# Four gated FFNs on one core: the second pair of chunks of each done whole like the first, x's sums cut into pieces, norms and low parts queued ahead of a step's evacuation

## The chip, the cores and the metric

The program runs on one core of a Trainium2 chip. The metric is the device time of one execution in microseconds (us). The engines of the core are TensorE (PE, with its weight loads shown as PEld), VectorE (DVE), ScalarE (ACT), GpSimd (POOL) and SyncE (SP), which issues the loads of the weights. Each engine works through its own queue in the order in which the program wrote it.

## The reference, cut to what matters

Two blocks of two layers each are computed on 512 tokens of width 1024. The change touches only the four gated FFNs of the second block:

```python
def rmsnorm_2(x, g, eps=EPS):
    y = x * lax.rsqrt(jnp.mean(x * x, axis=-1, keepdims=True) + eps)
    return y * g

def swiglu(h, w_gate, w_up, w_down):           # h: 512 x 1024, w_gate, w_up: 1024 x 2816
    return (jax.nn.silu(h @ w_gate) * (h @ w_up)) @ w_down

for layer in range(2):
    ...                                        # shared keys and values before layer 1
    x = x + 0.5 * swiglu(rmsnorm_2(x, ffn1_norm[layer]), ...)
    ...                                        # a recurrent block, or differential attention
    x = x + 0.5 * swiglu(rmsnorm_2(x, ffn2_norm[layer]), ...)
```

## The kernel before

x is kept transposed, in eight tiles of 128 features by 512 tokens (xT). Every fp32 operand of a product is split into a high part and a low part, and a product is three matmuls: high weights by high x, high weights by low x, low weights by high x (`fm`, L317 to L321). The high part of a weight block (wh) is a copy on ACT (L132), the low part (wl) a subtraction on DVE (L135). An FFN has 22 chunks of 128 hidden features, taken as 11 pairs, in the groups `PAIRS` of two, two, two, two and three pairs. The four FFNs have the keys a, b, c and d; each is one call of `swiglu`.

A pair can be done in two ways. Done **whole** (`sw_first`, pair 0 alone), each of its two chunks takes two products of 24 matmuls with 512 columns, one for the gate and one for the up weights; DVE multiplies the two results by the tokens' norm rB (L515), ACT takes the silu, DVE multiplies (L517), and ACT and DVE make the high and the low part of the result z (L518, L519). Done **in seven steps** (`step`, all other pairs), the 1024 inputs and the 512 tokens are halved, and seven products of 24 matmuls with 256 columns replace the eight of a plain product by halves (Winograd's form). Steps 1, 2, 4 and 5 read sums and differences of parts of x instead of x. `x_sums` makes these in four calls, on DVE (L482, L483, L487 to L489, L491, L492) and ACT (L484 to L486, L490), and in the kernel before all four stand in `sw_first`. The weights of steps 1, 2, 4 and 6 are sums too: one DVE addition of 128x1024 each (L454), then the copy on ACT, then the low part on DVE.

What each step leaves in PSUM is taken out right after it: for steps 0, 1 and 2 an ACT copy (`keep`, L574), for steps 3, 4 and 5 DVE operations (L582, L586, L588), for step 6 an ACT copy (L590). Steps 0, 2, 4 and 6 add up in one PSUM bank, so step 2 can't start before the copy of step 0 is out. When the seven are done, three things finish the pair (`end`): `scaled` (two DVE multiplications by rB, L600, each followed by an ACT silu, L601), `both` (a DVE product, L604, and the ACT copy that makes z's high part, L606) and `low` (z's low part on DVE, L609). They wait in the list `todo`; each following step takes one off after its matmuls are written.

Between the steps of a group stand the eight **downs** of the group before (`sw_down`): 12 matmuls with 512 columns each, then a DVE operation that adds the result to xT (L534). `sw_items` says after which steps they stand. The last group's downs (18 matmuls each) stand behind the last pair.

The weights come through one stream (`Stream`): `get` for an item splits the item two places on into its parts, from raw blocks that SP has loaded. With `late=True` the low part is not written to DVE's queue at once but kept in a list, which `flush` empties; in the kernel before a step and a down call `flush` after their evacuation, at their very end:

```python
            product(r, w, x, k0, c, s in (0, 1, 3), s in (3, 5, 6))
            if todo:
                todo.pop(0)()
            ...                       # evacuation of the step
            else:
                nc.scalar.activation(zf[:, :, 0, hi], q, AF.Copy)
                todo.extend(end(p, zf))
                todo.pop(0)()
            self.ws.flush()
```

## Time and profile before

| | us |
|---|---|
| median of 3 runs | 3972.29 (3971.31 to 3974.96) |
| profiled execution | 3975.06 |
| its span, on the core | 3973.3 |
| PE busy in the span | 3694.2 (93%) |
| DVE, ACT, POOL busy | 2670.4 (67%), 1604.9 (40%), 720.0 (18%) |

The four FFNs lie at 1930.04 to 2321.34 us of the span (a), 2505.91 to 2888.89 (b), 2980.82 to 3365.44 (c) and 3579.11 to 3963.27 (d); each from the first matmul of its first whole product to the end of its last down. The span is the core's time from its first instruction to its last; what the profiled execution adds to it is 1.8 us.

How to read the views: PE's matmuls overlap, so a matmul's own duration is longer than the distance to the next one, and lengths are taken here from start to start. An entry in square brackets in the order of time is the time that the engine sat idle before the row, and what ended it. In a row of a window the number behind each engine is its busy time in the stretch and in brackets its instructions; PEclk is the granted share of TensorE's clock.

### The profile page before, as it was taken

How to read it: one execution, taken by the hardware profiler on the slowest of the kernel's cores; microseconds unless marked ns; L12 is line 12 of the kernel's file. 1: busy time of each engine (PE TensorE's matmuls, PEld its weight loads, DVE VectorE, ACT ScalarE, POOL GpSimd, SP SyncE). 2: the span in 40 equal slices, each digit the busy share in tenths (PEclk: the TensorE clock that was granted, in tenths of full speed). 3: DMA queues.
4: the chain of work that ended last, by engine and by line, in shares of the span. 5: the costliest groups of instructions: out<-in, count | busy, mean ns of one | idle time of the engine just before them, and what ended most of it. 6: DMA issues, size and time to landing. Idle time of an engine off the chain costs nothing.

```text
span 3973.3 us, 55166 instructions
## 1 busy us (share of the span) xinstructions
PE 3694.2 (93%) x21404; PEld 3198.1 (80%) x21404; DVE 2670.4 (67%) x4329; ACT 1604.9 (40%) x2642; POOL 720.0 (18%) x755
## 2 busy tenths in 40 slices
PE   7999989999999879999899988899998999998998
PEld 5887978888877778887688866788877888677887
DVE  7887787665554395444677767677756776766775
ACT  2454422222234484233344445444434444564443
POOL 5433230000021282000100034000030000550000
PEclk8999999999999999999899999999999999899999
DMA  5300043344413532333233323233353333213332
GB/s 180 95 1 22 14 130 116 111 127 121 120 50 105 156 110 78 94 89 92 66 103 95 93 67 90 75 96 96 96 152 88 96 98 99 75 48 88 96 96 77
DMA packets 586147, 367.72 MB, mean 93 GB/s; under 512 B 34487, under 2 KB 563373, under 8 KB 585885
## 3 DMA queue, kind: packets, MB, share of 16 engines
q1 hardware_dynamic: 564573, 348.31, 29.9%
q0 software_dynamic: 3520, 9.59, 0.8%
q10 hardware_dynamic: 17792, 6.29, 0.7%
q8 instruction: 169, 2.77, 0.3%
q14 instruction: 93, 0.76, 0.1%
HBM read 347.82 MB, written 16.30 MB: 92 GB/s over the span
## 4 chain that ended last, share of the span: by engine, by line
PE 64%; DVE 19%; ACT 7%; issue 6%; DMA 3%; POOL 1%; SPq 0%; DVEq 0%; ACTq 0%; POOLq 0%
PE D L1483 6%; PE D L317 5%; PE D L319 5%; PE D L321 5%; DVE wl L135 5%; PE D L551 3%; PE D L549 3%; PE D L550 3%; PE M L531 3%; PE M L532 3%; PE M L530 3%; PE V L1928 2%; DVE ws L454 2%; ACT wh L132 2%; PE E L549 2%
## 5 line engine op out<-in xcount | busy, mean ns | idle before, releaser
L135 DVE TENSOR_TENSOR wl<-ws,wh 128x1024 fp32r<-128x1024 f32 (+3 forms) x502 | 621.4, 1246 | 269.2 <-ACT wh L132 268.2
L132 ACT ACTIVATE wh<-ws 128x1024 fp32r<-128x1024 f32 (+3 forms) x502 | 486.7, 984 | 722.0 <-DVE ws L454 399.0
L551 PE MATMUL D<-ah,wl 128*128 128x256 f32 x1440 | 411.2, 286 | 48.9 <-DVE wl L135 48.0
L549 PE MATMUL D<-ah,wh 128*128 128x256 f32 x1440 | 407.3, 283 | 13.8 <-ACT t L574 13.8
L550 PE MATMUL D<-al,wh 128*128 128x256 f32 x1440 | 405.6, 282 | 0.0
L551 PEld LDWEIGHTS D<-ah,wl 128*128 128x128 f32 x1440 | 273.7, 190 | 58.8 <-DVE wl L135 58.8
L530 PE MATMUL M<-hz,wh 128*128 128x512 f32 x704 | 282.3, 401 | 8.6 <-ACT hz L606 8.6
L549 PEld LDWEIGHTS D<-ah,wh 128*128 128x128 f32 x1440 | 273.9, 190 | 20.2 <-ACT t L574 16.3
L531 PE MATMUL M<-hz,wh 128*128 128x512 f32 x704 | 282.5, 401 | 2.7 <-DVE hz L609 2.7
L532 PE MATMUL M<-hz,wl 128*128 128x512 f32 x704 | 281.8, 400 | 0.0
L550 PEld LDWEIGHTS D<-al,wh 128*128 128x128 f32 x1440 | 273.7, 190 | 4.1
L341 POOL TENSOR_TENSOR acc<-acc,t 128x512 f32<-128x512 f32 x36 | 46.9, 1302 | 1233.7 <-ACT t L340 1233.7
L549 PE MATMUL E<-ah,wh 128*128 128x256 f32 x800 | 227.2, 284 | 19.2 <-ACT t L574 9.7
L551 PE MATMUL E<-ah,wl 128*128 128x256 f32 x800 | 229.0, 286 | 14.1 <-DVE wl L135 13.5
L550 PE MATMUL E<-al,wh 128*128 128x256 f32 x800 | 225.9, 282 | 0.0
L303 POOL TENSOR_TENSOR hl<-t,hh 128x768 fp32r<-128x768 f32 (+1 forms) x44 | 69.2, 1573 | 811.0 <-ACT hh L302 770.1
L317 PE MATMUL D<-ah,wh 128*128 128x512 f32 (+1 forms) x512 | 205.8, 402 | 6.4 <-DVE G L797 4.2
L321 PE MATMUL D<-ah,wl 128*128 128x512 f32 (+1 forms) x512 | 203.9, 398 | 2.5 <-DVE wl L135 2.5
L319 PE MATMUL D<-al,wh 128*128 128x512 f32 (+1 forms) x512 | 203.7, 398 | 0.3 <-POOL al L2625 0.2
L1300 DVE SCALAR_TENSOR_TENSOR as<-ws,S,as 128x256 f32<-128x256 f32 x448 | 198.5, 493 | 4.9 <-DMA ws<-in_ada_w_dram 1.4
L317 PE MATMUL D<-x7h,wh 128*128 128x512 f32 (+1 forms) x464 | 183.5, 398 | 3.0 <-ACT x7h L2620 1.6
L319 PE MATMUL D<-x7l,wh 128*128 128x512 f32 (+1 forms) x464 | 181.9, 395 | 1.0 <-POOL x7l L2625 0.5
(707 smaller groups left out, 9767.5 us busy)
## 6 DMA issues: line engine op xcount, KB each, us to landing
ws<-in_ffn_w_up_dram SPq DMA_DIRECT2D x96, 512.0 KB
ws<-in_ada_w_dram SPq DMA_DIRECT2D x88, 512.0 KB
t<-in_ffn_w_down_dram SPq DMA_DIRECT2D x128, 256.0 KB
ws<-in_ffn_w_gate_dram SPq DMA_DIRECT2D x80, 256.0 KB
ws<-in_ffn_w_up_dram SPq DMA_DIRECT2D x80, 256.0 KB
wz<-in_ffn_w_gate_dram SPq DMA_DIRECT2D x80, 256.0 KB
wz<-in_ffn_w_up_dram SPq DMA_DIRECT2D x80, 256.0 KB
ws<-in_ffn_w_down_dram SPq DMA_DIRECT2D x32, 384.0 KB
```

The source lines that it names most:

```text
L132: self.nc.scalar.activation(h[:, :n], t[:, :n], AF.Copy)
L135: self.nc.vector.tensor_tensor(l[:, :n], t[:, :n], h[:, :n], ALU.subtract)
L317: nc.tensor.matmul(o, wh[:, kw + k], xh[:, k0 + k, s], start=a, stop=False)
L319: nc.tensor.matmul(o, wh[:, kw + k], xl[:, k0 + k, s], start=False, stop=False)
L321: nc.tensor.matmul(o, wl[:, kw + k], xh[:, k0 + k, s], start=False, stop=z)
L530: nc.tensor.matmul(q, wh[:, k], z[:, 0, i], start=k == 0, stop=False)
L531: nc.tensor.matmul(q, wh[:, k], z[:, 1, i], start=False, stop=False)
L532: nc.tensor.matmul(q, wl[:, k], z[:, 0, i], start=False, stop=k == 2 * np_ - 1)
L549: nc.tensor.matmul(o, wh[:, u, k], xh(k0 + k, s), start=start and k == 0, stop=False, skip_group_check=True)
L550: nc.tensor.matmul(o, wh[:, u, k], xl(k0 + k, s), start=False, stop=False, skip_group_check=True)
L551: nc.tensor.matmul(o, wl[:, u, k], xh(k0 + k, s), start=False, stop=stop and k == 3, skip_group_check=True)
L1483: nc.tensor.matmul(o, w[u][:, k], hs[m0 + k][h][:, s], start=k == 0 and i == 0, stop=k == nm - 1 and i == 2)
```

## The change

Pairs 0 and 1, the whole first group, are done by `sw_first`; `sw_first` takes the pair as an argument. One call of `x_sums` belongs to each chunk of the two pairs. It is a generator now, and its three pieces are written at three places of the chunk: the first behind the gate product, the second behind the silu, the third behind the ACT copy of z's high part. Its scratch tile moves from a ring that the downs' weights use to the tile of the norm's diagonal. `flush` moves ahead of the evacuation, in the step and in the down. `scaled` is no longer taken off `todo` at the end of step 6, so that `scaled`, `both` and `low` come one step later each, in steps 0, 1 and 2 of the next pair; the buffer gu is asked for at step 3. In a group's second pair the first down stands behind step 0 and no longer behind step 1.

```diff
-                if p0 + q == 0:
+                if not gi:
                     for m in range(2):
-                        yield "g", 0, m
-                        yield "u", 0, m
+                        yield "g", q, 2 * q + m
+                        yield "u", q, 2 * q + m
                     continue
                 for s in range(7):
                     yield "s", p0 + q, s
-                    if down and s in ((2, 3, 5, 6), (1, 2, 4, 6))[q]:
+                    if down and s in ((2, 3, 5, 6), (0, 2, 4, 6), ())[q]:
                         yield down.pop(0)
...
     def x_sums(self, d, n):
-        t = self.tmp(TT, tag="ca", bufs=3)
+        t = self.tmp(TT, tag="diag", bufs=1)
         nc.vector.tensor_scalar(ng, gb, -1.0, None, ALU.mult)
         nc.vector.tensor_tensor(f, a0, a1, ALU.subtract)
         nc.scalar.activation(e, a1, AF.Copy, scale=g)
         nc.scalar.activation(f, f, AF.Copy, scale=g)
         nc.scalar.activation(th[:, 0:TC], f, AF.Copy)
+        yield
         nc.vector.scalar_tensor_tensor(t[:, TC:2 * TC], b1, gb, e, ALU.mult, ALU.subtract)
         nc.vector.scalar_tensor_tensor(t[:, 0:TC], b1, ng, f, ALU.mult, ALU.subtract)
         nc.vector.scalar_tensor_tensor(t[:, 2 * TC:], b0, ng, t[:, 0:TC], ALU.mult, ALU.subtract)
+        nc.vector.tensor_tensor(tl[:, 0:TC], f, th[:, 0:TC], ALU.subtract)
         nc.scalar.activation(th[:, TC:], t, AF.Copy)
-        nc.vector.tensor_tensor(tl[:, 0:TC], f, th[:, 0:TC], ALU.subtract)
+        yield
         nc.vector.tensor_tensor(tl[:, TC:], t, th[:, TC:], ALU.subtract)
...
-    def sw_first(self, key, d):
+    def sw_first(self, key, d, p):
...
-                self.fm([(q[:, i], slice(0, T))], self.ws.get((key, kind, 0, m)), d.x)
+                self.fm([(q[:, i], slice(0, T))], self.ws.get((key, kind, p, 2 * p + m)), d.x)
...
-                if m == 0 and i == 0:
-                    d.t = self.acts512()
-                else:
-                    self.x_sums(d, 2 * m + i - 1)
+                if not i:
+                    if not p and not m:
+                        d.t = self.acts512()
+                    x = self.x_sums(d, 2 * p + m)
+                    next(x)
             nc.vector.tensor_tensor(zf[:, :, m], q, d.rB.unsqueeze(1).to_broadcast([P, 2, T]), ALU.mult)
             nc.scalar.activation(zf[:, 0, m], zf[:, 0, m], AF.Silu)
+            next(x)
             nc.vector.tensor_tensor(zf[:, 1, m], zf[:, 0, m], zf[:, 1, m], ALU.mult)
             nc.scalar.activation(z[:, 0, m], zf[:, 1, m], AF.Copy)
+            next(x, None)
             nc.vector.tensor_tensor(z[:, 1, m], zf[:, 1, m], z[:, 0, m], ALU.subtract)
-        self.x_sums(d, 3)
         return z
...
     def sw_down(self, key, gi, n, hs, scale):
+        self.ws.flush()
         x = self.xT[:, n]
         nc.vector.scalar_tensor_tensor(x, q, scale, x, ALU.mult, ALU.add)
...
         def step(p, s, banks):
             if s == 0:
-                un[p] = dict(z=self.gu())
+                un[p] = {}
...
             if todo:
                 todo.pop(0)()
-            zf, q = d_["z"], r[:, :, lo]
+            self.ws.flush()
+            if s == 3:
+                d_["z"] = self.gu()
+            zf, q = d_.get("z"), r[:, :, lo]
...
                 todo.extend(end(p, zf))
-                todo.pop(0)()
-            self.ws.flush()
```

The order of the built programs shows what this moves. DVE, FFN a, from the last whole chunk's multiplication by rB (L515 before, L519 after) to the first seven-step pair. wl is a low part, L454 a weight sum, al a low part of x's sums, hz a low part of z. Before:

```order
L515 TENSOR_TENSOR gu_16686<-D_16789,rB_16765 128x2x512
L517 TENSOR_TENSOR gu_16686<-gu_16686 128x512
L519 TENSOR_TENSOR hz_16685<-gu_16686,hz_16685 128x512
L482 TENSOR_SCALAR t_16881<-VC 128x1
L483 TENSOR_TENSOR t_16882<-xT 128x256
L487 SCALAR_TENSOR_TENSOR t_16884<-xT,VC,t_16883 128x256
L488 SCALAR_TENSOR_TENSOR t_16884<-xT,t_16881,t_16882 128x256
L489 SCALAR_TENSOR_TENSOR t_16884<-xT,t_16881,t_16884 128x256
L491 TENSOR_TENSOR al_16734<-t_16882,ah_16733 128x256
L492 TENSOR_TENSOR al_16734<-t_16884,ah_16733 128x768
L135 TENSOR_TENSOR wl_16835<-ws_73,wh_16834 128x1024
L454 TENSOR_TENSOR ws_73<-ws_73,wz_16684 128x1024
```

After, behind the last chunk of pair 1:

```order
L519 TENSOR_TENSOR gu_16869<-E_16953,rB_16767 128x2x512
L489 SCALAR_TENSOR_TENSOR t_16984<-xT,VC,t_16983 128x256
L490 SCALAR_TENSOR_TENSOR t_16984<-xT,t_16981,t_16982 128x256
L491 SCALAR_TENSOR_TENSOR t_16984<-xT,t_16981,t_16984 128x256
L492 TENSOR_TENSOR al_16728<-t_16982,ah_16727 128x256
L522 TENSOR_TENSOR gu_16869<-gu_16869 128x512
L495 TENSOR_TENSOR al_16728<-t_16984,ah_16727 128x768
L525 TENSOR_TENSOR hz_16868<-gu_16869,hz_16868 128x512
L135 TENSOR_TENSOR wl_16993<-wz_16682,wh_16992 128x1024
L454 TENSOR_TENSOR wz_16682<-wz_16682,ws_74 128x1024
```

Behind the last L515 of before stood one whole call of `x_sums` after z's low part, and ahead of it in the same queue another; behind the last L519 of after stand two pieces of one call, among z's own operations. The low part L135 is that of step 1 of the first seven-step pair in both.

DVE, from the last evacuation of one seven-step pair (L588 before, L597 after) into the next pair, which is the first of its group (pair 3 into pair 4, FFN a). Before:

```order
L588 SCALAR_TENSOR_TENSOR gu_17444<-D_16897,t_17551 128x2x256
L600 TENSOR_TENSOR gu_17444<-gu_17444,rB_16765 128x2x512 x2
L135 TENSOR_TENSOR wl_17693<-ws_73,wh_17692 128x1024
L454 TENSOR_TENSOR ws_73<-ws_73,wz_16683 128x1024
L534 SCALAR_TENSOR_TENSOR xT<-M_17729,xT 128x512
L135 TENSOR_TENSOR wl_17727<-ws_73,wh_17726 128x1024
L454 TENSOR_TENSOR ws_73<-ws_73,wz_16684 128x1024
L604 TENSOR_TENSOR gu_17444<-gu_17444 128x1024
L135 TENSOR_TENSOR wl_17746<-ws_73,wh_17745 128x1024
```

After:

```order
L597 SCALAR_TENSOR_TENSOR gu_17504<-E_17032,t_17453 128x2x256
L135 TENSOR_TENSOR wl_17595<-wz_16682,wh_17594 128x1024
L454 TENSOR_TENSOR wz_16682<-wz_16682,wz_16683 128x1024
L135 TENSOR_TENSOR wl_17625<-wz_16682,wh_17624 128x1024
L540 SCALAR_TENSOR_TENSOR xT<-M_17627,xT 128x512
L454 TENSOR_TENSOR wz_16682<-wz_16682,ws_74 128x1024
L607 TENSOR_TENSOR gu_17504<-gu_17504,rB_16767 128x2x512 x2
L135 TENSOR_TENSOR wl_17644<-wz_16682,wh_17643 128x1024
L135 TENSOR_TENSOR wl_17678<-t_17538,wh_17677 128x512
L611 TENSOR_TENSOR gu_17504<-gu_17504 128x1024
```

The low parts of the next pair's steps 0 and 1 now stand ahead of the norms (L600 before, L607 after) and of the down's addition to xT (L534, now L540); the norms stand behind the weight sum of step 2.

ACT at the same place, from the copy of step 6 (L590, now L599) to the copy of step 0 (L574, now L583). Before:

```order
L590 ACTIVATE gu_17444<-D_16896 128x2x256
L601 ACTIVATE gu_17444<-gu_17444 128x512 x2
L132 ACTIVATE wh_17726<-ws_73 128x1024
L132 ACTIVATE wh_17745<-ws_73 128x1024
L606 ACTIVATE hz_17774<-gu_17444 128x1024
L574 ACTIVATE t_17776<-E_16898 128x512
```

After:

```order
L599 ACTIVATE gu_17504<-D_17031 128x2x256
L132 ACTIVATE wh_17624<-wz_16682 128x1024
L132 ACTIVATE wh_17643<-wz_16682 128x1024
L608 ACTIVATE gu_17504<-gu_17504 128x512 x2
L583 ACTIVATE t_17675<-D_17030 128x512
L132 ACTIVATE wh_17677<-t_17538 128x512
L613 ACTIVATE hz_17710<-gu_17504 128x1024
```

The copy of step 0 no longer stands behind the copy of z's high part (L606, now L613); the two silus stand ahead of it instead.

## Rows read from the trace of the kernel before

**Rows 1.** The page: PE's busy time, and its costliest group that waits.

```profile
PE 3694.2 (93%) x21404; PEld 3198.1 (80%) x21404; DVE 2670.4 (67%) x4329; ACT 1604.9 (40%) x2642; POOL 720.0 (18%) x755
L551 PE MATMUL D<-ah,wl 128*128 128x256 f32 x1440 | 411.2, 286 | 48.9 <-DVE wl L135 48.0
```

**Rows 2.** Windows, from:to and length: FFN a, one step, one whole product.

```profile
1930.04:2321.34 391.30, 360.41 (x2315) 323.01 (x2314) 289.59 (x355) 164.02 (x224) 14.64 (x14) 0.97 0.32 90
2077.50:2080.32 2.82, 2.82 (x25) 2.81 (x24) 1.82 (x2) 0.71 (x1) 0.00 (x0) 1.00 0.00 1
2980.82:2986.43 5.61, 5.61 (x26) 4.52 (x24) 1.21 (x2) 3.99 (x5) 0.00 (x0) 1.00 0.50 187
```

**Rows 3.** Windows: last whole product and pair 1's steps 0 to 2, FFNs a to d.

```profile
1958.55:1986.41 27.86, 15.99 (x98) 14.48 (x96) 20.70 (x32) 13.49 (x22) 0.00 (x0) 0.82 0.00 1
2524.53:2553.74 29.21, 17.71 (x97) 15.58 (x96) 21.40 (x34) 13.93 (x23) 0.00 (x0) 0.82 0.00 1
2998.53:3029.48 30.95, 18.68 (x97) 17.17 (x96) 22.12 (x35) 14.97 (x23) 0.00 (x0) 0.72 0.00 0
3597.74:3627.85 30.11, 16.39 (x97) 14.88 (x96) 21.40 (x34) 14.95 (x23) 0.00 (x0) 0.77 0.00 1
```

**Rows 4.** Windows: pair 2's steps 1, 2; pair 4's steps 0 to 2; pair 5's 0, 1.

```profile
2000.49:2009.17 8.68, 6.24 (x51) 5.83 (x49) 7.74 (x8) 5.19 (x7) 0.00 (x0) 1.00 0.05 15
2063.70:2074.70 11.00, 9.30 (x74) 8.67 (x72) 9.44 (x10) 5.61 (x7) 0.00 (x0) 1.00 0.06 17
2097.19:2103.93 6.74, 6.20 (x50) 5.79 (x49) 6.18 (x7) 2.56 (x4) 0.00 (x0) 1.00 0.11 34
```

**Rows 5.** In order of time, PE, FFN a: matmuls that waited (start, length).

```profile
1979.53 0.58 PE L551 MATMUL D<-ah,wl 128*128 128x256 f32 x1 [11.87 <-DVE wl L135]
...
2071.78 0.39 PE L549 MATMUL E<-ah,wh 128*128 128x256 f32 x1 [1.18 <-ACT t L574]
```

**Rows 6.** Groups by line, DVE, 1950 to 1979.5 us: x's sums.

```profile
L492 DVE TENSOR_TENSOR al<-t,ah 128x768 fp32r<-128x768 f32 x4 | 3.8, 958 | 2.3 <-ACT ah L490 2.3
...
L487 DVE SCALAR_TENSOR_TENSOR t<-xT,VC,t 128x256 f32<-128x256 f32 x4 | 1.9, 483 | 3.1 <-ACT t L484 3.1
...
L491 DVE TENSOR_TENSOR al<-t,ah 128x256 fp32r<-128x256 f32 x4 | 1.7, 418 | 0.0
```

**Rows 7.** In order of time, DVE, where pair 3 ends and pair 4 begins.

```profile
2061.73 1.23 DVE L600 TENSOR_TENSOR gu<-gu,rB 128x1024 f32<-128x1024 f32 x1 [1.15 <-ACT gu L590]
2062.87 1.22 DVE L135 TENSOR_TENSOR wl<-ws,wh 128x1024 fp32r<-128x1024 f32 x1
2064.12 1.22 DVE L454 TENSOR_TENSOR ws<-ws,wz 128x1024 f32<-128x1024 f32 x1
2065.26 0.68 DVE L534 SCALAR_TENSOR_TENSOR xT<-M,xT 128x512 f32<-128x512 f32 x1
2066.47 1.22 DVE L135 TENSOR_TENSOR wl<-ws,wh 128x1024 fp32r<-128x1024 f32 x1 [0.53 <-ACT wh L132]
2067.73 1.23 DVE L454 TENSOR_TENSOR ws<-ws,wz 128x1024 f32<-128x1024 f32 x1
2068.87 1.22 DVE L604 TENSOR_TENSOR gu<-gu 128x1024 f32<-128x1024 f32 x1
```

**Rows 8.** The same place, ACT.

```profile
2061.10 0.60 ACT L590 ACTIVATE gu<-D 128x512 f32<-128x512 f32 x1 [2.77 <-PE D L551]
2061.59 0.63 ACT L601 ACTIVATE gu<-gu 128x512 f32<-128x512 f32 x1
...
2068.99 1.06 ACT L132 ACTIVATE wh<-ws 128x1024 fp32r<-128x1024 f32 x1 [2.55 <-DVE ws L454]
2070.18 1.06 ACT L606 ACTIVATE hz<-gu 128x1024 fp32r<-128x1024 f32 x1
2071.15 0.58 ACT L574 ACTIVATE t<-E 128x512 f32<-128x512 f32 x1
```

**Rows 9.** Window around the end of FFN a's last pair.

```profile
2280.00:2295.00 15.00, 12.09 (x56) 9.67 (x56) 10.17 (x11) 5.52 (x8) 0.00 (x0) 0.89 0.28 80
```

More of the change, by code (lines that the diff above doesn't have):

```diff
@@ L615, in swiglu @@
         for kind, a, b in items:
-            if kind == "g" and b == 0:
-                hs[0] = self.sw_first(key, d)
-                three = [self.bank("D"), self.bank("D"), self.bank("E")]
+            if kind == "g" and b % 2 == 0:
+                hs[a] = self.sw_first(key, d, a)
+                if a == 1:
+                    three = [self.bank("D"), self.bank("D"), self.bank("E")]
             elif kind == "s":
@@ L630, in swiglu @@
                 self.sw_down(key, a, b, hs, 0.5)
-                self.ws.flush()
                 if a == last and on_x:
```

## The prediction

> **What bounds the kernel now.** I read the page first: PE is busy 93% of the span, and the costliest group of its matmuls that waits, waits for low parts of weights from DVE [rows 1]. So a change pays only where it shortens PE's own work or a wait of PE. Then I cut PE's order of time at the starts of the FFNs' products and took the windows. One step of 24 matmuls with 256 columns takes 2.82 us, one whole product of 24 with 512 columns 5.61 [rows 2]; a down of 12 with 512 columns is half of that, 2.81. Nearly everything in an FFN runs at these rates with nothing lost. What is lost lies at a few places, and I count it as window less its products at full rate:
>
> - Pair 0 into pair 1: each window holds one whole product and three steps, 5.61 + 3 x 2.82 = 14.06 us. They took 27.86, 29.21, 30.95 and 30.11 [rows 3]: lost 13.8, 15.15, 16.9 and 16.05, together 61.9. In FFN a 11.87 of it is one wait, for a low part [rows 5]. DVE is busy 20.70 of the 27.86 us and stood in a queue with two calls of x's sums. The rest, 13.8 - 11.9 = 1.9, comes after the wait: the granted clock of these windows is 0.72 to 0.82 of the full 2.4 GHz, so part of each ran at 1.2.
> - Pair 1 into pair 2: 8.68 for two steps [rows 4], lost 3.05.
> - Into the first pair of a group (pairs 4, 6, 8, and 10 likewise): 11.00 for three steps [rows 4], lost 2.55.
> - Into the second pair of a group (pairs 3, 5, 7, 9): 6.74 for two steps [rows 4], lost 1.11.
> - Behind the last pair PE waits for z: of 15 us it is busy 12.09, at 0.89 of the clock [rows 9].
>
> In the four FFNs that is 61.9 + 12.2 + 40.8 + 17.8 = 132.7 us, without starts and ends, which the change leaves alone.
>
> **Pair 1 whole.** Seven steps become four products: 4 x 5.61 - 7 x 2.82 = +2.7 us of PE per FFN, on the path, +10.8 in all. The bytes loaded are the same. Per column the two kinds of matmul cost the same here: a whole product has twice the columns of a step and takes 1.99 times as long [rows 2].
>
> The Trainium skill ("Perfetto Trace Analysis", Optimizing Tensor Performance) holds larger matmuls to be more efficient than smaller ones, and the Trainium skill ("TensorE: Matmul & The Clock Gate", Back-to-back issue gap) gives each a fixed cost of some 2.5 ns beside its columns; by these the charge would be some 2.4 us an FFN (an estimate: 96 x 215.8 - 168 x 109.2 ns), and the sum 1 us lower. The rows show 2.7, and decide.
>
> **x's sums in pieces.** A call has DVE operations of 0.96, 3 x 0.48 and 2 x 0.42 us [rows 6], near 3.3 with the small one, plus waits for ACT (2.3 and 3.1 in four calls). Before, four stood around two chunks; now one stands in each of four, 11.2 us of PE apiece. A chunk's DVE work is two low parts and the multiplication by rB at 1.22, two half ones at 0.69 and the 3.3: 8.4 of 11.2. So DVE keeps up and the loss of pair 0 into pair 1 goes: **-61.9**.
>
> What is late next is the end of pair 1. The low part for step 1 of pair 2 stands behind the last chunk's tail. DVE begins some 0.2 after PE goes on (a matmul lasts 286 ns [rows 1], the next starts 117 after it [rows 2]); multiplication by rB 1.13 (starts follow 1.13 to 1.14 apart [rows 7]), three sums and a low part 1.7 (3 x 0.48 + 0.42, overlapping a little), a product 0.6, then x's low part, which waits for an ACT copy of 768 columns (between 0.6 and 1.06 [rows 8]) and starts near 4.0 and z's low part at 4.9; the weight's low part runs 5.5 to 6.7. Step 1 wants it at 2.82 + 0.23 = 3.05: 3.6 lost. Then weight sum, copy and low part of step 2 (1.23 + 1.06 + 1.22 with 0.04 between) against another 3.05: 0.6 more. I take 4.3. In a and d step 0 needs the same bank as the last chunk and takes 1.5 of the same wait. After waits like these PE ran slower for a while (1.9 above, 0.89 in [rows 9]): 0 to 2, I take 1.4. So 5.7 in place of 3.05: **+10.5**. Bounds: 3 (what pair 2 loses now [rows 4]) and 7.1 (one more wait for ACT of [rows 6], 0.8, in the tail, and 2 for the clock).
>
> **Norms and low parts ahead.** Count from the start of step 0 of the next pair; durations from [rows 7, 8].
>
> *First pair of a group* (steps 0, 1, 2, then a down). The low parts of steps 0 and 1 are now done before step 0 begins. DVE: addition to xT at 0.2, weight sum of step 2 at 0.8, norms at 1.94 and 3.07, low part of step 2 from 4.2 to 5.4, wanted at 5.87. ACT: weight copy 2.06 to 3.12, silus to 3.83 and 4.96, copy of step 0 4.9 to 5.5; step 2 starts at 5.63 and needs it. Before, that copy stood behind z's high part (L606) and ended at 2071.73 [rows 8], and PE waited 1.18 for it [rows 5]. So nothing is lost here; z's low part (L604, copy, L609 behind that) comes at 15.9 and the down, which starts at 14.1, wants it with its eighth matmul at 15.7: 0.2 to 0.3 lost. 0.3 for 2.55, three times per FFN: **-27**. In the last pair, with no downs between its steps, step 6 wants the bank of step 4 2.8 us after step 4, and step 4's evacuation (2 x 0.42 on DVE) now stands behind step 6's weight sum, copy and low part; by the same count it comes 0.6 late. 0.7 for 2.55, four times: **-7.4**.
>
> *Second pair of a group* (0, down, 1, 2, down, 3, 4). The chain is the same to 5.4, but then come: weight sum of step 2 at 5.46, copy 6.72, low part 7.82 to 9.04, wanted at 8.67 (0.43 late). DVE: addition at 8.95, a down's low part, L604 10.15 to 11.37. ACT: z's high part to 12.47, copy of step 1 to 12.98, and only then the weight copy of step 3, to 13.95; its low part ends at 15.2, wanted at 14.8 (0.45). Sum, copy and low part of step 4 end at 18.7, wanted at 18.2 (0.57). With some 0.1 for starting again each time: 1.75 lost for 1.11, sixteen times: **+10**. The third down, moved behind step 0, is what covers step 1 here.
>
> The loads: raw blocks are given back at a flush, so no later than before; SP's queue gets nothing new, and the ring of the downs' weights loses x's sums as a user. I cost that at nothing; the DMA share over FFN a is 0.32 at 90 GB/s [rows 2]. The evacuations on DVE now stand behind a low part; elsewhere than in the last pair the bank of step 4 is wanted again 5.6 us on. Nothing too.
>
> **The sum.** -61.9 + 10.8 + 10.5 - 27 - 7.4 + 10 = -65 us. Against the profiled execution's 3975.06 (span 3973.3 and 1.8 around it) that gives 3910; this execution is 2.8 above the median of the runs, so the median should be 3972.3 - 65 = **3907**. The unknowns: the end of pair 1, 3 to 7.1 where I took 5.7 (-11 to +6); second pairs, 1.1 to 2.3 (-10 to +9); first pairs, 0 to 1.1 (-4 to +10). Not all fall on one side: 3892 to 3923 for this case.
>
> **The rivals.**
>
> - *The boundaries lose nothing.* ACT and DVE have slack over a pair (DVE is busy 289.59 of 391.30 us [rows 2]), and if the copies and low parts catch up the second pairs lose 0: 3907 - 28 - 4 - 3 = 3872. Against it: sum, copy and low part stand in series, 3.6 us, and a step has 2.82.
> - *The boundaries stay as they are.* The wait moves from one link to the next, first pairs lose 2.55 as now: 3907 + 27 + 7 - 10 = 3931. For it: the second pairs, where I find just that.
> - *The backlog moves to the end of pair 1.* If DVE can't keep up with x's pieces, pair 1 into pair 2 loses what pair 0 into 1 did, 15.5 for my 5.7: 3907 + 39 = 3946. Against it: 8.4 of 11.2.
> - *The blocks come late (slower).* The weight sums of steps 1 and 2 now stand ahead of the norms in DVE's queue. If a raw block is not in when its sum's turn comes, the norms, the silus and the copy of step 0 all stand behind it. The price is a block's load: 512 KB at the 187 GB/s of a busy stretch [rows 2] is some 2.8 us, an estimate, at 32 boundaries: 3907 + 90 = 3997. It decides when the block lands later than 0.8 us into step 0. No wait of that kind is in [rows 7]. The rows show DVE working in the written order, so nothing could pass the stalled sum.
> - *The change does nothing*, its order being undone when it is built: the order shows that it isn't. 3972.
>
> **How the numbers follow.** Forecast 0.72, boundaries free 0.08, boundaries as they are 0.08, backlog moved 0.07, late blocks 0.03, nothing 0.02. The range takes in the forecast's own and reaches to 3932, so that the boundaries as they are lie in it, and to 3889: some 0.2 is left out. A difference under 0.2% (8 us) can't be told from none here. Faster 0.95 (the first four), same 0.02, slower 0.03.
>
> **What the profile after would show.** Each FFN 14 to 19 us shorter, a near 377 for 391.3; no wait of 9 to 12 us of PE behind pair 0; a wait of 3 to 4 us, or of 1.5 and 2, at steps 0 and 1 of pair 2, with a lower clock behind it; no wait for the copy of step 0 (1.18 before) in pairs 4, 6 and 8; three waits of 0.4 to 0.6 for low parts at steps 2, 3 and 4 of pairs 3, 5, 7, 9. A wait over 5 us at pair 2 would make the pieces of x's sums wrong, DVE waiting for loads the last assumption, and waits of 2 us in pairs 4, 6, 8 the chain of norms.

## The result, and the profile after

The changed kernel took 3907.5 us (median of 4 runs, 3902.80 to 3910.74), the kernel before, on the same chip, 3971.8 (3969.15 to 3974.96): a ratio of 0.9837, 95% interval 0.982 to 0.9854. The forecast was 3907. The profiled execution has a span of 3904.1 us where before it was 3973.3: 69.2 less. The four FFNs, from the first matmul to the end of the last down, took 374.09, 367.93, 366.61 and 366.69 where they had taken 391.30, 382.98, 384.62 and 384.16: 67.7 of the 69.2 lie in them. One execution of e6_norms_only, at a granted clock of 0.75 where its others had 0.98, took 6378 us and is left out of its median below.

First the page of the kernel after, the lines that answer to [rows 1]:

```profile
PE 3693.3 (95%) x21116; PEld 3180.9 (81%) x21116; DVE 2622.7 (67%) x4293; ACT 1587.0 (41%) x2618; POOL 720.3 (18%) x755
L557 PE MATMUL D<-ah,wl 128*128 128x256 f32 x1344 | 382.6, 285 | 20.2 <-DVE wl L135 20.2
```

The same group of matmuls waits for the same low parts, 20.2 us in place of 48.0. PE's busy time is nearly the same: pair 1 whole adds work, and less time goes into slow running and into starting again behind waits, which count as busy ([rows 4] has 9.30 us busy for 8.45 of work).

Then windows of the kernel after (from:to, length, busy time of PE, PEld, DVE, ACT, POOL with their instructions, PEclk, DMA share, GB/s): FFN a; its last five whole products; then the last whole chunk's end to the end of step 2 of pair 2 in FFNs a, b, c and d.

```profile
1927.96:2302.05 374.09, 359.46 (x2243) 318.33 (x2242) 277.69 (x346) 159.27 (x218) 14.64 (x14) 0.99 0.33 94
1954.74:1982.83 28.09, 28.09 (x121) 22.41 (x119) 18.88 (x29) 13.58 (x21) 0.00 (x0) 1.00 0.46 122
...
1982.83:1995.67 12.84, 9.61 (x74) 8.83 (x74) 10.39 (x13) 5.62 (x8) 0.00 (x0) 1.00 0.08 24
...
2533.22:2546.66 13.44, 10.29 (x73) 10.08 (x72) 10.20 (x13) 5.71 (x8) 0.00 (x0) 0.87 0.12 36
2992.20:3006.70 14.50, 11.35 (x73) 11.14 (x72) 10.38 (x13) 5.71 (x8) 0.00 (x0) 0.76 0.18 54
3572.38:3585.14 12.76, 9.56 (x73) 8.80 (x73) 10.39 (x13) 5.61 (x8) 0.00 (x0) 1.00 0.07 21
```

The five products take 28.09 us, and five at the full rate are 5 x 5.61 = 28.05: nothing is lost where [rows 3] lost 13.8 to 16.9. DVE is busy 18.88 of the 28.09 and keeps up. Pair 2's steps 0 to 2 are 8.45 us at the full rate, so the boundary behind pair 1 loses 4.4, 5.0, 6.0 and 4.3. In a and d the granted clock is 1.00 and nearly all of it is waiting; in b and c it is 0.87 and 0.76, and 1.5 and 2.6 us of the loss are matmuls that ran at the lower level behind the wait.

Now a window of the second pair of a group (pair 3's steps 0 to 4 with the two downs between them), then two of the first pair of the next group (steps 0 to 2, and the down behind them), and one of the whole last pair (seven steps), all in FFN a:

```profile
2018.19:2039.66 21.47, 20.52 (x145) 18.81 (x144) 17.60 (x18) 9.91 (x13) 0.00 (x0) 1.00 0.20 58
...
2050.91:2059.42 8.51, 8.51 (x73) 8.51 (x72) 7.25 (x8) 3.93 (x6) 0.00 (x0) 1.00 0.06 17
2059.42:2062.46 3.04, 3.04 (x14) 2.18 (x13) 2.34 (x2) 2.90 (x5) 0.00 (x0) 1.00 0.73 212
...
2242.84:2263.35 20.51, 20.01 (x170) 19.84 (x168) 19.11 (x21) 10.34 (x13) 0.00 (x0) 1.00 0.05 16
```

The first pair loses 8.51 - 8.45 and 3.04 - 2.81, together 0.29, where [rows 4] had 2.55. The second pair loses 21.47 - (5 x 2.82 + 2 x 2.81) = 1.75, where it had 1.11. The last pair loses 20.51 - 7 x 2.815 = 0.8, where it had 2.55. The next rows show, in the order of time, PE's three waits in the second pair, DVE's chain there, and one piece of ACT's queue:

```profile
2027.28 0.38 PE L557 MATMUL D<-ah,wl 128*128 128x256 f32 x1 [0.26 <-DVE wl L135]
2033.40 0.39 PE L557 MATMUL D<-ah,wl 128*128 128x256 f32 x1 [0.24 <-DVE wl L135]
2036.94 0.39 PE L557 MATMUL D<-ah,wl 128*128 128x256 f32 x1 [0.46 <-DVE wl L135]
```

```profile
2019.00 1.22 DVE L454 TENSOR_TENSOR ws<-ws,wz 128x1024 f32<-128x1024 f32 x1
...
2022.40 1.22 DVE L135 TENSOR_TENSOR wl<-ws,wh 128x1024 fp32r<-128x1024 f32 x1
2023.65 1.23 DVE L454 TENSOR_TENSOR ws<-ws,ws 128x1024 f32<-128x1024 f32 x1
2026.00 1.23 DVE L135 TENSOR_TENSOR wl<-ws,wh 128x1024 fp32r<-128x1024 f32 x1 [1.12 <-ACT wh L132]
...
2032.12 1.23 DVE L135 TENSOR_TENSOR wl<-ws,wh 128x1024 fp32r<-128x1024 f32 x1 [0.21 <-ACT wh L132]
...
2035.66 1.23 DVE L135 TENSOR_TENSOR wl<-wz,wh 128x1024 fp32r<-128x1024 f32 x1 [1.18 <-ACT wh L132]
```

```profile
2029.60 1.06 ACT L613 ACTIVATE hz<-gu 128x1024 fp32r<-128x1024 f32 x1 [3.10 <-DVE gu L611]
2030.57 0.58 ACT L583 ACTIVATE t<-E 128x512 f32<-128x512 f32 x1
2031.04 1.05 ACT L132 ACTIVATE wh<-ws 128x1024 fp32r<-128x1024 f32 x1
```

Step 0 began at 2018.19. From there step 1's weight sum runs at 0.81 and its low part at 4.2, the weight sum of step 2 at 5.46, its low part at 7.81 and ends at 9.04: the prediction's count to within a hundredth. ACT makes z's high part before the weight copy of step 3, which is the second wait. Each low part ends a few hundredths before the matmul that wanted it.

### The profile page after: what moved, and what is told of

Same layout as the page of the kernel before. It is cut to its first block, busy times and chain, and to the rows that moved or that the text cites. A ratio compares the mean times of both kernels' runs of the same rounds, so it can differ in the third digit from the quotient of the medians.

```text
span 3904.1 us, 54600 instructions
## 1 busy us (share of the span) xinstructions
PE 3693.3 (95%) x21116; PEld 3180.9 (81%) x21116; DVE 2622.7 (67%) x4293; ACT 1587.0 (41%) x2618; POOL 720.3 (18%) x755
## 5 line engine op out<-in xcount | busy, mean ns | idle before, releaser
L135 DVE TENSOR_TENSOR wl<-ws,wh 128x1024 fp32r<-128x1024 f32 (+3 forms) x474 | 586.7, 1246 | 324.4 <-ACT wh L132 322.4
L132 ACT ACTIVATE wh<-ws 128x1024 fp32r<-128x1024 f32 (+3 forms) x474 | 457.3, 978 | 571.4 <-DVE ws L454 256.8
L557 PE MATMUL D<-ah,wl 128*128 128x256 f32 x1344 | 382.6, 285 | 20.2 <-DVE wl L135 20.2
L317 PE MATMUL D<-ah,wh 128*128 128x512 f32 (+1 forms) x616 | 246.0, 399 | 3.1 <-ACT wh L132 2.8
L321 PE MATMUL D<-ah,wl 128*128 128x512 f32 (+1 forms) x616 | 243.1, 395 | 2.8 <-DVE wl L135 2.8
L319 PE MATMUL D<-al,wh 128*128 128x512 f32 (+1 forms) x616 | 243.2, 395 | 0.3 <-POOL al L2632 0.2
L303 POOL TENSOR_TENSOR hl<-t,hh 128x768 fp32r<-128x768 f32 (+1 forms) x44 | 69.2, 1573 | 808.4 <-ACT hh L302 767.5
L557 PE MATMUL E<-ah,wl 128*128 128x256 f32 x672 | 189.9, 283 | 4.1 <-DVE wl L135 4.1
L555 PE MATMUL E<-ah,wh 128*128 128x256 f32 x672 | 188.9, 281 | 2.9 <-DVE gu L519 2.8
L556 PE MATMUL E<-al,wh 128*128 128x256 f32 x672 | 188.3, 280 | 0.0
L321 PE MATMUL D<-x7h,wl 128*128 128x512 f32 (+1 forms) x464 | 181.4, 394 | 1.1 <-DVE wl L135 1.1
```

The lines of the kernel that those rows point to most:

```text
L132: self.nc.scalar.activation(h[:, :n], t[:, :n], AF.Copy)
L135: self.nc.vector.tensor_tensor(l[:, :n], t[:, :n], h[:, :n], ALU.subtract)
L317: nc.tensor.matmul(o, wh[:, kw + k], xh[:, k0 + k, s], start=a, stop=False)
L319: nc.tensor.matmul(o, wh[:, kw + k], xl[:, k0 + k, s], start=False, stop=False)
L321: nc.tensor.matmul(o, wl[:, kw + k], xh[:, k0 + k, s], start=False, stop=z)
L555: nc.tensor.matmul(o, wh[:, u, k], xh(k0 + k, s), start=start and k == 0, stop=False, skip_group_check=True)
```

## The experiments

Each kernel ran with the kernel before on the same chip; ratios are to that.

| kernel | what it is | median us | ratio, 95% interval |
|---|---|---|---|
| after | the change | 3907.5 | 0.9837 (0.982 to 0.9854) |
| e1_whole | only pair 1 whole and x's pieces | 3929.6 | 0.9887 (0.9874 to 0.9901) |
| e2_order | only the reordering | 3946.7 | 0.9929 (0.9917 to 0.9942) |
| e3_old_places | after, the downs where they were | 3874.5 | 0.9751 (0.9738 to 0.9765) |
| e4_uncut | after, x's sums not cut | 3914.8 | 0.9848 (0.9835 to 0.9862) |
| e5_low_parts_only | e3, norms where they were | 3910.1 | 0.9837 (0.9824 to 0.985) |
| e6_norms_only | e3, low parts where they were | 3894.1 | 0.9799 (0.9785 to 0.9812) |
| e7_x_early | e3, x's sums ahead of the last tail | 3869.6 | 0.9745 (0.9732 to 0.9758) |
| e8_tail_later | e7, the last tail put off | 3858.6 | 0.9711 (0.9698 to 0.9724) |
| e9_down_moved_alone | before, the one down moved | 3961.2 | 0.9968 (0.9956 to 0.9979) |
| e10_last_pair | e8, the last pair by halves | 3861.0 | 0.9718 (0.9705 to 0.9731) |
| e11_last_pair_woven | e10, halves woven | 3841.9 | 0.9671 (0.9658 to 0.9685) |

**The two halves of the change.** My theory was the prediction's own: the gain is the sum of separate boundaries. The first experiment takes the reordering out:

```diff
-                    if down and s in ((2, 3, 5, 6), (0, 2, 4, 6), ())[q]:
+                    if down and s in ((2, 3, 5, 6), (1, 2, 4, 6), ())[q]:
...
             product(r, w, x, k0, c, s in (0, 1, 3), s in (3, 5, 6))
             if todo:
                 todo.pop(0)()
-            self.ws.flush()
...
                 todo.extend(end(p, zf))
+                todo.pop(0)()
+            self.ws.flush()
```

> Only the first half of the change: pair 1 whole and x's sums in pieces; norms, low parts and the third down stand where the kernel before has them. My theory counts the two halves apart: this one keeps -61.9 + 10.8 + 10.5 and gives back 27 + 7.4 - 10 = 24.4 against the changed kernel (3907.5): 3932. Its trace: no loss between pairs 0 and 1, first pairs of a group again 2.5 over their products, second pairs 1.1. Rival A, the reordering of norms and low parts does nothing: 3907. Rival B, the two halves need each other (without the early low parts the pieces of x's sums pile up at the end of pair 1): over 3950.

It took 3929.6. Windows of its pair 3 (steps 0, 1) and pair 4 (steps 0 to 2):

```profile
2021.35:2028.10 6.75, 6.17 (x50) 5.76 (x49) 6.19 (x7) 2.55 (x4) 0.00 (x0) 1.00 0.14 41
2053.40:2064.41 11.01, 9.25 (x74) 8.64 (x73) 9.44 (x10) 5.62 (x7) 0.00 (x0) 1.00 0.04 13
```

6.75 and 11.01 stand where [rows 4] has 6.74 and 11.00: these boundaries are untouched, and pair 0 into pair 1 loses nothing. The second one keeps the reordering and does pair 0 alone whole, with x's sums as before:

```diff
-                if not gi:
+                if p0 + q == 0:
...
-                    x = self.x_sums(d, 2 * p + m)
-                    next(x)
+                else:
+                    self.x_sums(d, 2 * m + i - 1)
```

> Only the second half: norms and low parts ahead of a step's evacuation and the third down of a second pair behind step 0; pair 0 alone is whole and x's sums are called as before. Theory: 3972 - 24 to 28 (the boundary of pairs 1 and 2 is now a first pair of its kind and gains 1 to 1.5 us in each FFN as well) = 3944 to 3948, with 13 to 17 us still lost between pairs 0 and 1. Rival A (the reordering does nothing): 3972. Rival B (the early low part of step 1 also breaks the wait between pairs 0 and 1): 3925 or less.

It took 3946.7, as expected. The gains alone, 1.13% and 0.71%, add to 1.84%, the change has 1.63%. At the boundary of pairs 1 and 2 the reordering gains some 1.5 us an FFN in e2, where pair 1 goes in steps. With pair 1 whole it gains nothing there: the losses behind pair 1 are 4.3, 5.0, 5.0 and 4.3 in e1, without the reordering, and 4.4, 5.0, 6.0 and 4.3 in the change.

**The moved down.** The prediction says that the third down, behind step 0, "is what covers step 1". I put it back behind step 1:

```diff
-                    if down and s in ((2, 3, 5, 6), (0, 2, 4, 6), ())[q]:
+                    if down and s in ((2, 3, 5, 6), (1, 2, 4, 6), ())[q]:
```

> The changed kernel with the downs of second pairs back behind steps 1, 2, 4 and 6 (the change put the first of them behind step 0). Counted through with the durations of the rows: with the norms ahead, the low part of step 1 is in time without that cover, and a down between steps 1 and 2 and another behind step 2 gives the chain of weight sum, copy and low part 5.6 us a step in place of 2.8 just where it is late. The three waits of 0.5 to 0.7 in pairs 3, 5, 7, 9 go, 16 x 1.75 = 28 us: 3879. Rival, as my prediction had it (the moved down covers step 1): step 1 then waits about a us in the 16 pairs: 3907 or slower.

It took 3874.5, 33 less than the change, and the intervals stand apart. Its window over the same steps of pair 3, and DVE's chain there:

```profile
2021.64:2041.33 19.69, 19.69 (x145) 18.60 (x144) 16.19 (x18) 8.73 (x12) 0.00 (x0) 1.00 0.23 68
```

```profile
2018.08 1.23 DVE L454 TENSOR_TENSOR ws<-ws,wz 128x1024 f32<-128x1024 f32 x1
2020.61 1.22 DVE L135 TENSOR_TENSOR wl<-ws,wh 128x1024 fp32r<-128x1024 f32 x1 [1.30 <-ACT wh L132]
...
2025.32 1.22 DVE L454 TENSOR_TENSOR ws<-ws,ws 128x1024 f32<-128x1024 f32 x1
2026.45 1.22 DVE L611 TENSOR_TENSOR gu<-gu 128x1024 f32<-128x1024 f32 x1
2027.87 1.23 DVE L135 TENSOR_TENSOR wl<-ws,wh 128x1024 fp32r<-128x1024 f32 x1 [0.20 <-ACT wh L132]
```

19.69 is the full rate, PE busy in all of it. The low part of step 1, the second of these rows, ends 0.2 us into step 0, so nothing at step 1 needs cover. Step 2 begins at 2030.08 and its low part, the last row, ends at 2029.10: weight sum, copy and low part are 3.6 us in series, and with the down behind step 1 they fit. The three waits, together 1.75, are gone from all 16 pairs: 28 of the 33 us. In the profiled executions the four FFNs are 31.7 us shorter; 3.5 of these lie where the waits are the same in both and fewer matmuls ran slowly behind them.

The stream explains the difference. It splits an item two places on, and a down is an item like a step. With the down behind step 1, step 1 is split in the last down of the pair before, and its weight sum runs at 2018.08, 3.6 us ahead of step 0. With the down behind step 0, step 1 is split in step 0 itself: in the change its sum runs 0.8 us into step 0, its low part stands behind the norms and is ready 5.4 us in, and the weight sum of step 2 behind that. So the moved down does cover step 1 there, which would otherwise want the low part at 3.05, but only from a lateness that the move itself brought.

Was the move a mistake from the start? I made it alone in the kernel before:

```diff
-                    if down and s in ((2, 3, 5, 6), (1, 2, 4, 6))[q]:
+                    if down and s in ((2, 3, 5, 6), (0, 2, 4, 6))[q]:
```

> The kernel before, with nothing changed but the third down of second pairs, which goes from behind step 1 to behind step 0. In that order the norms stand in step 6 of the pair before, and what second pairs lose (0.3 at step 0, 0.8 at step 1) is late at step 1: the down moved ahead of it gives the low part 2.8 us more, the 0.8 go, 16 times: 3972 - 13 = 3959. Rival, the moved down costs by itself what it cost in the changed kernel (e3_old_places was 33 faster without it): 3985 or more. If the first holds, the same move is worth -13 in the old order and +33 in the new one.

It took 3961.2: 13 faster. In the old order the late low part is step 1's, and there the move does cover it: in e9 second pairs lose 0.4 to 0.6 where they had 1.1, and nothing of it at step 1. So the same edit changes the time by -13 us in one order and by +33 in the other. The norms, moved in the same change, had taken the wait away that it was made for: e6_norms_only below, with the downs in their old places, loses nothing in second pairs.

**The cut of x's sums.** All three pieces go behind the second product of their chunk, ahead of its tail (the multiplication by rB, the silu, the product and z's two parts):

```diff
-                    x = self.x_sums(d, 2 * p + m)
-                    next(x)
+                else:
+                    for x in self.x_sums(d, 2 * p + m):
+                        pass
...
-            next(x)
...
-            next(x, None)
```

> The changed kernel with x's sums not cut: each whole call stands behind the second product of its chunk, ahead of the chunk's tail. Theory: pair 1 whole is what gives four gaps for four calls, and a call, 3.3 us of DVE and 2 to 3 of waiting for ACT, fits into a product of 5.6, so the cut is worth little: step 1 of pair 2 even starts 0.7 earlier, 3 us in all: 3904 to 3908. Rival (the cut is what keeps DVE from standing in a call ahead of the tail): a wait of 0.8 to 3 for each of the four chunks of an FFN: 3920 to 3955.

My theory missed, and so did the rival's price: 3914.8. The ratio's interval overlaps that of the change, so the time alone doesn't settle it; the places do. Between pairs 0 and 1 nothing is lost, as in the change, so the gain of 61.9 there comes from four calls having four whole chunks, and the cut isn't needed for it. Behind pair 1 the FFNs lose 4.2, 6.8, 6.9 and 6.9, 5 more than the change in all. FFN a also loses 1.6 more at its start, but it does so in e10_last_pair too, where the sums are cut. DVE in FFN b, around the end of the last chunk at 2534.77, and PE's wait:

```profile
2532.88 0.15 DVE L483 TENSOR_SCALAR t<-VC 128x1 f32<-128x1 f32 x1
...
2536.87 0.96 DVE L495 TENSOR_TENSOR al<-t,ah 128x768 fp32r<-128x768 f32 x1 [0.58 <-ACT ah L493]
2537.74 1.22 DVE L520 TENSOR_TENSOR gu<-D,rB 128x1024 f32<-128x1024 f32 x1
...
2541.65 1.22 DVE L135 TENSOR_TENSOR wl<-wz,wh 128x1024 fp32r<-128x1024 f32 x1
```

```profile
2542.93 0.58 PE L556 MATMUL D<-ah,wl 128*128 128x256 f32 x1 [4.92 <-DVE wl L135]
```

And DVE and PE of the kernel after, where the chunk ends at 2533.22:

```profile
2533.42 1.23 DVE L519 TENSOR_TENSOR gu<-D,rB 128x1024 f32<-128x1024 f32 x1 [3.45 <-PE D L321]
```

```profile
2539.62 0.39 PE L557 MATMUL D<-ah,wl 128*128 128x256 f32 x1 [3.15 <-DVE wl L135]
```

With the pieces DVE has been idle for 3.45 us and starts the tail 0.2 behind the product; with whole calls it is still in the call, and starts 3.0 behind. A call is 3.3 us of work, but with its waits for ACT this one holds DVE's queue for 5, from 2532.88 on. The Trainium skill ("Perfetto Trace Analysis", Optimizing Scalar/DVE Operations) says that where these engines aren't saturated but make others wait, breaking up instructions can let work finish sooner. DVE is busy 67% here and makes PE wait, but what is cut is a run of instructions and no single one, so this run doesn't test that; e10_last_pair and e11_last_pair_woven below do break up instructions, and gain only when woven. The pieces are worth some 5 us here.

**Norms and low parts apart.** Both on e3. In e5 the norms go back to step 6, in e6 the flush back behind the evacuation, in the step as shown and in the down likewise:

```diff
                 todo.extend(end(p, zf))
+                todo.pop(0)()
```

> e3_old_places (3874.5) with the norms back in step 6 of their own pair; the low parts stay ahead of the evacuation. It takes the two reorderings apart; with neither, e1_whole took 3929.6. Counted through with the durations of the rows: first pairs of a group and the last pair wait 1.75 at step 1 or 2, since the copy of step 0 stands behind both silus and they behind two norms that now precede the weight sums, second pairs 0.4. Against 0.25 and 0.7 in e3 that is some 7.5 more in each FFN: 3905. Rival A, the norms' place is worth nothing: 3875. Rival B, the low parts' place is worth nothing without the norms': 3930.

```diff
                 todo.pop(0)()
-            self.ws.flush()
...
                 todo.extend(end(p, zf))
+            self.ws.flush()
```

> e3_old_places (3874.5) with the low parts back behind the evacuation; the norms stay in step 0 of the next pair. Counted through: second pairs lose nothing, first pairs 1.2 at step 1 and 0.3 at the down, the last pair 1.3: some 4.2 more in each FFN: 3891. Rival A, the low parts' place is worth nothing: 3875. Rival B, the norms' place is worth nothing without the low parts': 3930. If e5 and e6 come as counted, the two gains (25 and 38 us of 55) overlap, because they shorten one chain.

They took 3910.1 and 3894.1, 5 and 3 above the count. At the boundaries the count holds: first pairs lose 1.77 and 1.56 against 2.56 with neither and 0.27 with both, second pairs 0.35 and 0 against 1.1. In the profiled executions the four FFNs are 33.8 and 17.9 us longer than in e3, for 30 and 16.8 counted; most of what is over is slow running behind waits that e3 has as well. In all, by the ratios, 20 and 35 us from e1 add up to the 54 of both. I had said that they overlap. They do in second pairs, where the norms alone take all of 1.1, and in first pairs it is the other way: 0.8 and 1.0 alone, 2.3 together.

**The end of pair 1.** It is the other place where the change loses more than the kernel before. First x's sums and the late low part ahead of the last chunk's tail, and a bank for step 0 that the last chunk doesn't use:

```diff
+            if p and m:
+                for _ in x:
+                    pass
+                self.ws.flush()
             nc.vector.tensor_tensor(zf[:, :, m], q, d.rB.unsqueeze(1).to_broadcast([P, 2, T]), ALU.mult)
...
-                    three = [self.bank("D"), self.bank("D"), self.bank("E")]
+                    three = [self.bank(t) for t in ("DED" if self.nd % 3 == 0 else "DDE")]
```

> e3_old_places, and in the last whole chunk alone x's sums are finished, and the late low part given out, ahead of the multiplication by rB; the three banks of the steps are taken in an order in which step 0 never needs the last chunk's. Theory: the wait at step 1 of pair 2 (3.15, or 1.4 and 1.5) was the low part behind the chunk's tail and goes; step 2 then waits some 2.2 to 2.6 for its own weight sum, copy and low part, which still stand behind the tail. 1.5 less in each FFN, and less slow running: 3864 to 3870. Rival (as in e4_uncut, more of x's sums ahead of the tail makes the tail late): 3875 to 3882.

It took 3869.6; the ratio doesn't separate it from e3, but the wait moved as expected: none at steps 0 and 1, and at step 2 this one of PE, with DVE's rows ahead of it (FFN b):

```profile
2532.70 0.41 PE L559 MATMUL E<-ah,wh 128*128 128x256 f32 x1 [1.95 <-ACT t L587]
```

```profile
2529.80 1.22 DVE L454 TENSOR_TENSOR wz<-wz,ws 128x1024 f32<-128x1024 f32 x1
2532.20 1.22 DVE L135 TENSOR_TENSOR wl<-wz,wh 128x1024 fp32r<-128x1024 f32 x1 [1.18 <-ACT wh L132]
```

The weight sum of step 2 stands behind the whole tail; ACT's copy of step 0 (L587) stands behind the copy of that sum. The four places behind pair 1 lose 15.1 where e3 lost 18.6. So the tail is what has to move: the product and z's two parts go to steps 0 and 1, as in other pairs.

```diff
-            nc.vector.tensor_tensor(zf[:, 1, m], zf[:, 0, m], zf[:, 1, m], ALU.mult)
-            nc.scalar.activation(z[:, 0, m], zf[:, 1, m], AF.Copy)
-            next(x, None)
-            nc.vector.tensor_tensor(z[:, 1, m], zf[:, 1, m], z[:, 0, m], ALU.subtract)
+            if p and m:
+                todo.extend((high, low))
+            else:
+                high()
+                next(x, None)
+                low()
```

> e7_x_early, and the last chunk's product, z's high part and z's low part are put off: they go out in steps 0 and 1 of pair 2, as the norms do in other pairs. Theory: the weight sum of step 2 then stands right behind the multiplication by rB: 0.2 + 1.14 + 1.23 + 1.06 + 1.22 is 4.9 us into pair 2, and step 2 wants it at 5.9, so the pair loses nothing and the 4.3 to 6 us of each FFN are gone: 3853 to 3858. Rival A (the wait goes on to step 3 or to the first down, which needs z): 3862 to 3870. Rival B, the wait is for another thing than that chain: as e7.

It took 3858.6. Windows of steps 0 to 2 of pair 2 in FFNs a and b, and DVE in b:

```profile
1988.15:1996.66 8.51, 8.51 (x73) 8.51 (x72) 7.48 (x8) 4.65 (x7) 0.00 (x0) 1.00 0.07 20
2528.30:2536.84 8.54, 8.54 (x73) 8.54 (x72) 7.51 (x8) 4.66 (x7) 0.00 (x0) 1.00 0.07 20
```

```profile
2529.29 1.22 DVE L523 TENSOR_TENSOR gu<-D,rB 128x1024 f32<-128x1024 f32 x1
2530.42 1.22 DVE L454 TENSOR_TENSOR wz<-wz,ws 128x1024 f32<-128x1024 f32 x1
...
2532.83 1.23 DVE L135 TENSOR_TENSOR wl<-wz,wh 128x1024 fp32r<-128x1024 f32 x1 [0.59 <-ACT wh L132]
```

The weight sum now follows the multiplication by rB at once, and 12.84 to 14.50 us have become 8.5: the full rate. These places gain 14.7 us over e7 and the time only 11: in the profiled execution the first two downs behind the last pair took 6.9 more than in e7, with the same waits (see the last section).

**The last pair.** The waits left are those behind pair 10, as in [rows 9]. One more step in the same manner: z by halves.

```diff
                 nc.vector.scalar_tensor_tensor(zf[:, :, 1, lo], q, -1.0, d_.pop("u"), ALU.mult, ALU.subtract)
+                if p == sum(PAIRS[-1]) - 1:
+                    hs[p] = self.hz()
+                    half(p, zf, 1)
...
-                todo.extend(end(p, zf))
+                todo.extend(end(p, zf) if p < sum(PAIRS[-1]) - 1 else [lambda: half(p, zf, 0)])
```

> e8_tail_later (3858.6), and in the last pair the half of z that needs only steps 4 and 5 is finished while step 6 runs; the half that needs step 6 comes last in the downs' sums. Theory: the wait of 2.15 at the first down and the slow running behind it (3.5 to 6.1 us in each FFN) come from the chain copy, two norms, two silus, product of both halves, high part; with one half it is 0.2 + 0.6 + 1.14 + 0.63 + 0.6 + 0.63 = 3.8 us behind step 6, wanted at 3.5: 0.3 left. 3 to 4.5 less in each FFN: 3841 to 3847. Rival (low parts of the downs' weights now stand behind z's half on VectorE and are late instead): 3853 to 3862.

It took 3861.0, no gain: the rival's time, but not by its cause. PE waits for no low part of a down; it waits for z. The rows of DVE and PE in FFN b, where step 6 ends at 2791.13:

```profile
2789.59 1.23 DVE L623 TENSOR_TENSOR gu<-gu,rB 128x1024 f32<-128x1024 f32 x1
...
2793.70 0.96 DVE L135 TENSOR_TENSOR wl<-t,wh 128x768 fp32r<-128x768 f32 x1
2794.57 1.22 DVE L623 TENSOR_TENSOR gu<-gu,rB 128x1024 f32<-128x1024 f32 x1
```

```profile
2797.89 0.51 PE L551 MATMUL M<-hz,wh 128*128 128x512 f32 x1 [3.10 <-ACT hz L626]
```

The second half's multiplication starts 3.4 us behind step 6, for the first half's chain and a down's low part stand ahead of it. Woven, only the multiplication of the first half is ahead:

```diff
-                    half(p, zf, 1)
+                    norm(zf, 1)
...
+            norm(zf, 0)
+            silu(zf, 0)
+            for m in (1, 0):
+                nc.vector.tensor_tensor(zf[:, 1, m], zf[:, 0, m], zf[:, 1, m], ALU.mult)
+                nc.scalar.activation(z[:, 0, m], zf[:, 1, m], AF.Copy)
+            for m in (1, 0):
+                nc.vector.tensor_tensor(z[:, 1, m], zf[:, 1, m], z[:, 0, m], ALU.subtract)
```

> As e10_last_pair, with the same two halves of z, but woven together: e10's trace shows the first half's whole chain, 4.1 us on VectorE with 1.5 of it spent waiting for ScalarE, and a down's low part of 0.96, in front of the second half, so that z's high part came 6.7 us behind step 6 where e8_tail_later had 5.1. Here only the first half's multiplication by rB stands ahead of step 6's weight work, its silu beside step 6, and the products and high parts of both halves follow the second half's multiplication. Theory: z's last high part comes 3.8 us behind step 6; with 12 matmuls of 0.234 and then two waits of 0.3 to 0.8 PE loses 1 to 1.5 where e8 loses 3 (2.15, 0.76) and 0.5 to 2 of slow running: 8 to 14 us in the four FFNs, 3845 to 3851. Rival (the downs' weight work on VectorE and ScalarE fills that place, whatever the order): 3857 to 3862.

It took 3841.9, less than expected. DVE and PE at the same place:

```profile
2787.13 0.95 DVE L135 TENSOR_TENSOR wl<-t,wh 128x768 fp32r<-128x768 f32 x1
2788.39 1.22 DVE L624 TENSOR_TENSOR gu<-gu,rB 128x1024 f32<-128x1024 f32 x1 [0.31 <-ACT gu L620]
```

```profile
2790.94 0.50 PE L551 MATMUL M<-hz,wh 128*128 128x512 f32 x1 [0.41 <-ACT hz L635]
2791.67 0.50 PE L552 MATMUL M<-hz,wh 128*128 128x512 f32 x1 [0.23 <-DVE hz L637]
```

The first two downs lose 1.3 in each FFN, where e8 lost 5.0 to 6.1, and behind these short waits no matmul ran slowly. Of the 17 us some 9 are waits and 8 are slow running that e8 had behind its longer ones; I had put that at 0.5 to 2 an FFN, and it was 1.5 to 2.7. This version beats both kernels: 0.9671 of the time before.

## Why the prediction was right, step by step

| step | predicted us | measured us |
|---|---|---|
| pair 0 into 1 | -61.9 | -61.9 (28.09 for 28.05 of work) |
| pair 1 whole | +10.8 | +10.8 (products at 5.61, steps at 2.82) |
| end of pair 1 | +10.5 | +7.5 (lost 4.4, 5.0, 6.0, 4.3, for 12.2 before) |
| first pairs of a group | -27 | -27 (0.29 for 2.55) |
| last pair | -7.4 | -7.1 (0.8 for 2.55) |
| second pairs | +10 | +10 (1.75 for 1.11) |
| sum | -65 | -67.7 by these places, -67.7 in the FFNs |

- The gain is where it was said to be, and e1 and e2 give it in two parts that add up but for the boundary behind pair 1. Two places that the table leaves out nearly cancel: FFN a was 1.7 us shorter at its start, and the downs of the last group lost 1.3 more.
- The step that was off in size is the end of pair 1, 5.7 an FFN for 4.3 to 6.0. Of this I had counted 4.3 as waits. In a and d the waits are 4.4 and 4.3, with the wait for the last chunk's bank (1.41 measured, 1.5 forecast) as counted. In b and c they are 3.5: the low part of step 1 was ready half a microsecond sooner (3.15 of wait, not 3.6), because x's third piece had not waited for ACT there, and step 2 did not wait, its low part being ready while matmuls still ran slowly. The slow running, for which I took 1.4 everywhere, was none in a and d (granted clock 1.00) and 1.5 and 2.6 in b and c: two waits of 1.4 and 1.5 cost less than one of 3.15.
- The median's 3907.5 is nearer to the forecast than the terms deserve: 3 us of the end of pair 1, the 2.8 by which the profiled execution of before lay above the median, and the 1.6 by which that of after lay below it, partly cancel.
- One sentence of the working was misleading, though its number was right: that the moved down is what covers step 1. It covers only the lateness that it causes. It is the cause of the +10, and of 18 more that were to be had; e3 shows it. I had counted the second pairs in the changed order only and never in that order with the downs where they had been. The rival "the boundaries lose nothing", 3872, was put aside because sum, copy and low part take 3.6 us and a step has 2.82. But the weights are split two items on, so in a second pair the chain has a step and a down, 5.6. In e3, where only the first pairs and the last one still lose 0.3 and 0.8, that is enough, and it took 3874.5.
- The other rivals: no backlog at the end of pair 1 (e4 shows what it looks like when the calls aren't cut, and its price is some 5 us, not 39); no late blocks (in the four FFNs DVE waits for no load); the boundaries did not stay as they were.

## What to carry to other kernels

When the order of one engine's queue changes, count every hand-placed cover again: a filler that was put in front of the late operation is in the wrong place once another operation is late, and it can cost more than it had brought. Ask also what the move does to the program's own look-ahead: here it made the next weights a place later. Count a boundary as one chain over two engines (here sum on VectorE, copy on ScalarE, low part on VectorE) against the work of TensorE that lies between; and put off whatever nobody needs soon until the chain is through. Cutting work into pieces paid here only where the pieces were woven in behind the chain that others wait for: halves written one after the other brought nothing, the same halves woven 17 us.

## What the runs showed of the hardware

Equal waits are followed by unequal slow running, that is, by matmuls at the lower of the two clock levels (in the kernel after, matmuls of 256 columns then start 0.21 us apart and not 0.12). PE waits 2.15 us for z in the first down of the last group in the kernel after and in e7 alike. The windows of the first two of these downs in FFN a, of the kernel after:

```profile
2263.35:2276.75 13.40, 10.49 (x39) 7.86 (x37) 7.34 (x8) 5.52 (x8) 0.00 (x0) 0.87 0.24 71
```

and of e7_x_early:

```profile
2255.49:2267.36 11.87, 8.95 (x39) 6.71 (x38) 7.31 (x8) 5.52 (x8) 0.00 (x0) 1.00 0.26 77
```

Busy times of DVE and ACT are the same, the granted clock is 0.87 in one and 1.00 in the other, and PE is busy 1.5 us longer for the same matmuls. Over the four FFNs what is lost to slow running there was 1.5, 2.6, 1.5 and 2.5 us in the kernel after, 0, 0, 0 and 1.3 in e7, and 2.5, 1.5, 2.7 and 1.5 in e8_tail_later, all behind the same wait. Behind waits of 3.15 at pair 2 it was 1.5 and 2.6, behind 1.41 and 1.51 none (granted clock 1.00), and behind the 1.18 us waits of e1 none. Nor does it simply grow with the wait: behind the 11.87 us of [rows 5] it was 1.4. What decides it is not shown by these runs. A sum over boundaries is therefore uncertain by two or three microseconds at each long wait.
